# Wider modulation strips and another order for the opening of a two-layer diffusion backbone

## The chip, the cores and the metric

The kernel runs on one core of a Trainium2 chip. A core has a matrix engine (TensorE, with its weight loads), VectorE, ScalarE, GpSimd and SyncE, which mostly issues transfers; the engines run their own instructions in order and wait for each other by semaphores. Transfers from HBM into the on-chip memory (SBUF) run on 16 DMA engines beside them. TensorE writes into PSUM, from where VectorE and ScalarE read. The metric is the device time of one execution in microseconds (us); lower is better.

## The reference

One inference step of two layers over 1024 latent tokens and 128 context tokens of width 1024, all in float32. Every layer starts with the same adaptive modulation:

```python
def ada_modulate(x, cond, norm_g, w_ada, b_ada):
    m = jax.nn.silu(cond) @ w_ada + b_ada
    shift, scale, gate = jnp.split(m, 3, axis=-1)
    h = rms_norm(x, norm_g) * (1.0 + scale[:, None, :]) + shift[:, None, :]
    return h, gate[:, None, :]
```

There are two conditions, one for the latent and one for the context tokens, so `silu(cond) @ w_ada` is a product of 2 rows with a 1024 x 3072 matrix. Layer 0 then projects h by one wide matrix and feeds two head groups: a Conformer convolution (GLU, a depthwise convolution of width 31, LayerNorm, swish) and a neighbourhood attention with the context keys in the same softmax. Their gated outputs go through one output projection. Layer 1 is a pooling mixer with a gate and an output projection. Each layer adds its gated output to its input.

## The kernel before, in words

**Precision.** Large products are made from two parts: a value is rounded to a short form (hi), the rest (lo) is kept, and three matmuls hi·hi, hi·lo and lo·hi stand for one. `split` does this for weights (ScalarE rounds, L186; VectorE subtracts, L187). `h_chunk` (from L442) does it for the modulated input: three transposes on TensorE (L445), scale and shift on ScalarE (L450), the rounding on VectorE (L451), the subtraction on GpSimd for even chunks and on VectorE for odd ones (L452).

**Groups and chunks.** The 9 token tiles of 128 form three groups of 384 tokens: group 0 is tiles 0 to 2, group 1 tiles 3 to 5, group 2 tiles 6, 7 and the context. The width 1024 is 8 chunks of 128 (k). A chain (`chain_ws`, L230) runs over the 8 chunks with three matmuls each into one bank of PSUM. `norm_x` makes the RMS norm of a tile: a Square with a sum on ScalarE (L126), two small steps on GpSimd (L113, L114), a scaling on VectorE (L128).

**Modulation.** The silu of both conditions lies in `sc`, one column for each condition and chunk. Layer 0's shift and scale are made in four steps m = 0 to 3, each for two chunks: `ada0_rows` multiplies four strips of 128 columns of the modulation's weights by the two conditions (L327). The stationary operand is `sc` (2 columns), the moving one the weights, and the four strips run side by side in the array's four groups of 32 columns, so that their results stand in rows 0-1, 32-33, 64-65 and 96-97 of a bank. VectorE copies these rows into `ads` (L333), which was zeroed before; `ada0_cols` transposes it (L338) and makes SH and SC (L273 to L279), which h_chunk needs. The other strips (layer 0's gate and all of layer 1) run later in the background through `ada_strips` (L360) and `ada_cols` (L383, L385, L391).

**The opening.** `first_chains` interleaves the first chains with the loading: the strips m, the chunks T(k, g) of groups 0 and 1, and the chain pieces C(k, ...) for two column blocks of weights x on group 0, written (0, 0) and (1, 0), and for block 0 on group 1, (0, 1). Its order is written out by hand: inside `tc.manual_schedule` TensorE, ScalarE and VectorE run in the program's order. SyncE's and GpSimd's order, and everything outside, is laid out by the planner from its own costs. The first half of the weights' chunks (u = 0, chunks 0 to 3) and the second half (u = 1) are split by `split_w0(c, u)`; the first split stands ahead of this order.

**Buffers that couple steps.** Transposes and strips share two banks of PSUM ("tp"), so a strip or chunk waits until the one before last is read out. The slots of x6 and x7 hold weights of the last modulation step, so these tiles are loaded when the strips of m = 3 have used them.

**Behind the opening** come the remaining projections of layer 0, with the convolution's taps in the background (VectorE L566; ScalarE L553 and GpSimd L555), attention, the output projection, and layer 1.

Of the kernel before, what the change touches and what calls it, by code (L numbers as in the profile page):

```python
# [10 lines left out]
F32 = mybir.dt.float32  # L11
F32R = mybir.dt.float32r
AF = mybir.ActivationFunctionType
ALU = mybir.AluOpType
AX = mybir.AxisListType
P = 128
# [3 lines left out]
G = 384  # L20
# [26 lines left out]
def _body(tc, nc, A, O, const, wp, arena, tmpp, smp, psp):  # L47
# [31 lines left out]

    ident = const.tile([P, P], F32, name="ident")  # L80
    make_identity(nc, ident)
    mhalf = const.tile([P, 16], F32, name="mhalf")
    gp.memset(mhalf, -0.5)
    corr = {}
    for w in (2, 4, 8, 16):
# [19 lines left out]
    xt = {}  # L105
# [35 lines left out]
    se.activation(th0, V[:, :16], AF.Tanh, scale=0.5)  # L141
    cu = small(16, "cu")
    ve.scalar_tensor_tensor(cu, th0, 1.0, V[:, :16], ALU.add, ALU.mult)
    sc = const.tile([P, 8, 2], F32, name="sc")
    ve.tensor_scalar(sc.rearrange("p k c -> p c k"), cu.rearrange("p (c k) -> p c k", c=2), 0.5, None, ALU.mult)

    vq = const.tile([P, 12], F32, name="vq")
    qn8, lgh, lbh = vq[:, 0:1], vq[:, 1:5], vq[:, 5:9]
# [41 lines left out]
    def load_raw0(c, u):  # L190
        wi = A["w_in_0"]
        mem = slot((18, 20)[c], name="raw")[:, :WUNIT] if u else None
        return load_raw([wi[:, c * P : (c + 1) * P], wi[:, 512 + c * P : 512 + (c + 1) * P]], (4 * u,), mem)[0]
# [87 lines left out]

    WAS = (0, 1, 4, 5, 2, 3, 6, 7, 8, 9, 10, 11, 16, 21, 22, 23)
    ads = [const.tile([P, P], F32, name=f"ads{i}") for i in range(2)]
    for t in ads:
        gp.memset(t, 0.0)
    for t in range(3):
        norm_x(t)
    first_w, wt = {}, {}
# [1 line left out]
    def load_wada(m):  # L290
        for kh in range(2):
            for x in range(2):
                t = slot(WAS[4 * m + 2 * kh + x], name="wada")[:, :D].rearrange("p (k c) -> p k c", c=256)
                c0 = x * D + m * 256
                sy.dma_start(t, A["w_ada_0"][kh * 512 : (kh + 1) * 512, c0 : c0 + 256].rearrange("(k p) c -> p k c", p=P))
                wt[m, kh, x] = t
                if m and late:
                    sy.dma_start(*late.pop(0))
# [3 lines left out]
    def split_w0(c, u):  # L302
        first_w[c, u] = split(*raw0[c, u])

    load_wada(0)
    raw0[0, 0] = load_raw0(0, 0)
    raw0[1, 0] = load_raw0(1, 0)
    for t in range(3, 6):
        load_x(t)
    load_wada(1)  # L310
    load_wada(2)
    raw0[0, 1] = load_raw0(0, 1)
    raw0[1, 1] = load_raw0(1, 1)
    load_wada(3)
    for t in (6, 7):
        load_x(t)
    split_w0(0, 0)
    adb = {}

    def ada0_rows(m):  # L320

        b = adb[m] = bank("tp")
        for k in range(8):
            for x in range(2):
                for q in range(2):
                    r = 32 * (2 * x + q)
                    te.matmul(  # L327
                        b[r : r + 2, :P], sc[:, k, :], wt[m, k // 4, x][:, k % 4, q * P : (q + 1) * P],
                        start=(k == 0), stop=(k == 7), tile_position=(0, r),
                    )  # L330
        t = ads[m % 2]
        for r in range(0, P, 32):
            ve.tensor_copy(t[r : r + 2, :], b[r : r + 2, :P])  # L333

    def ada0_cols(m):

# [11 lines left out]
    def ada_strips(l, col, n, fin):  # L348

        st = {}  # L350

        def step(k):
            w = slot(ADS[st_i[0] % len(ADS)], name="wad")[:, : 4 * n]
            st_i[0] += 1
            dma_later(w, A[f"w_ada_{l}"][k * P : (k + 1) * P, col : col + 4 * n])
            if k == 0:
                st["b"] = bank("tp")
            for q in range(4):
                r = 32 * q
                te.matmul(  # L360
                    st["b"][r : r + 2, :n], sc[:, k, :], w[:, q * n : (q + 1) * n],
                    start=(k == 0), stop=(k == 7), tile_position=(0, r),
                )
            if k == 7:
                st["then"] = fin(st["b"])


        then, owed_turn[:] = list(owed_turn), [lambda: st["then"] and st["then"]()]
        adq.append(then + [lambda k=k: step(k) for k in range(4)])
        adq.append([lambda k=k: step(k) for k in range(4, 8)])  # L370
# [8 lines left out]
    def ada_cols(l, b, c0):  # L379

        t = slot(ADS[st_i[0] % len(ADS)], name="adr")[:, :G]
        st_i[0] += 1
        gp.memset(t[:98, :], 0.0)  # L383
        for r in range(0, P, 32):
            ve.tensor_copy(t[r : r + 2, :], b[r : r + 2, :G])  # L385
        return lambda: ada_turn(l, t, c0)

    def ada_turn(l, t, c0):
# [50 lines left out]
        for k in range(8):  # L439
            h_chunk(g, src, l, hs, k, "tp" if k % 2 == 0 else "cv")  # L440

    def h_chunk(g, src, l, hs, k, tag):  # L442
        b = bank(tag)
        for i in range(3):
            te.transpose(out=b[:, i * P : (i + 1) * P], in_=src[i][:, k * P : (k + 1) * P], identity=ident)  # L445
        hi, lo = hsl(hs, 0, k, g), hsl(hs, 1, k, g)
        t = tmp("h")
        for a, e, c in ((0, G, 0),) if g < 2 else ((0, 256, 0), (256, G, 1)):
            s, o = SC[l][:, k, c : c + 1], SH[l][:, k, c : c + 1]
            se.activation(t[:, a:e], b[:, a:e], AF.Identity, bias=o, scale=s)  # L450
        ve.tensor_copy(hi, t[:, :G])  # L451
        (ve if k % 2 else gp).tensor_tensor(lo, t[:, :G], f(hi), ALU.subtract)  # L452

    def hslots(ids):
        return [
            tuple(slot(i, F32R, "h").rearrange("p (k t) -> p k t", t=G) for i in ids[2 * kh : 2 * kh + 2]) for kh in range(2)
        ]

    h0 = {}
# [7 lines left out]
    def first_chains():  # L467


        bs = {(0, 0): (bank("mm"), bank("mm")), (1, 0): (bank("mm"), bank("mm")), (0, 1): (bank("cv"), bank("cv"))}  # L470

        def C(k, which=((0, 0), (1, 0), (0, 1))):
            for x, g in which:
                w = [first_w[x, 0], first_w.get((x, 1))]
                for i in range(2):
                    chain_ws(bs[x, g][i][:, :G], w, i * P, h0, g, ks=(k,))

        def T(k, g):
            h_chunk(g, [xt[t] for t in range(3 * g, 3 * g + 3)], 0, h0, k, "tp")

        h0[0] = hslots(range(4))
        ada0_rows(0)
        ada0_cols(0)
        T(0, 0)
        T(1, 0)
        for k in range(2):
            C(k, ((0, 0),))
        split_w0(1, 0)
        for t in range(3, 6):
            norm_x(t)  # L490
        h0[1] = hslots(range(4, 8))
        for k in range(2):
            C(k, ((1, 0),))
        T(0, 1)
        T(1, 1)
        ada0_rows(1)
        for k in range(2):
            C(k, ((0, 1),))
        ada0_cols(1)
        for k in (2, 3):  # L500
            for g in range(2):
                T(k, g)
        for m in (2, 3):
            ada0_rows(m)
            C(2 * m - 2)
            ada0_cols(m)
            T(2 * m, 0)
            T(2 * m, 1)
            if m == 2:
                split_w0(0, 1)  # L510
            C(2 * m - 1, ((0, 0), (1, 0)))
            T(2 * m + 1, 0)
            T(2 * m + 1, 1)
            if m == 2:
                split_w0(1, 1)
            C(2 * m - 1, ((0, 1),))
        for x in bs:
            for k in (6, 7):
                C(k, (x,))
        return bs  # L520
# [955 lines left out]
```

## Time and profile before

| | us |
|---|---|
| median of 3 runs | 968.03 (967.97 to 968.07) |
| the profiled execution's own time | 967.94 |
| its span in the profile | 966.2 |
| busy in the span: TensorE matmuls | 941.5 |
| VectorE | 603.1 |
| ScalarE | 403.7 |
| GpSimd | 368.9 |

The profile is of one execution. Lines of the profile name an engine (PE is TensorE's matmuls, PEld its weight loads, DVE VectorE, ACT ScalarE, POOL GpSimd, SP SyncE), a line of the kernel, the operation, the tile written and the tiles read, shapes, a count, and in the timeline the start and the duration in us, then in brackets how long the engine had been idle before and what it waited for. A matmul's duration runs to its modelled end and overlaps the next one, so the pace of matmuls is read from their starts. A busy TensorE is therefore also not TensorE at its peak.

### The profile page before, as it was taken

What the parts mean: (1) busy time and instruction counts of PE and PEld (TensorE: products, weight loads), DVE (VectorE), ACT (ScalarE), POOL (GpSimd) and SP (SyncE); (2) the same over time, 40 slices, a digit from 0 to 9 for tenths busy, and PEclk for the clock granted to TensorE, in tenths of its full rate; (3) what the DMA queues carried; (4) which work ended last, traced back from release to release, by engine and by line L of the source; (5) the groups of instructions that cost most, each with busy time, mean ns of one, the idle gap of its engine ahead of it and who ended that gap; (6) DMA issues with size and microseconds to landing.
All of it is one profiled execution on the core that took longest, in us unless ns stands there. A gap on an engine that the chain in (4) does not pass through costs nothing.

```text
span 966.2 us, 16658 instructions
## 1 busy us (share of the span) xinstructions
PE 941.5 (97%) x6388; PEld 864.2 (89%) x6388; DVE 603.1 (62%) x1243; ACT 403.7 (42%) x815; POOL 368.9 (38%) x485
## 2 busy tenths in 40 slices
PE   4999999999999999999999999999999999999998
PEld 2899998899999999987777888889999999998887
DVE  3658999999683444457778447656335455585332
ACT  4365667775611344258876323353222222231010
POOL 2354879999944201125466246530000000004231
PEclk9999999999999999999999999999999999999999
DMA  9956945416111111135344312341111011133211
GB/s 311 308 194 145 363 182 185 160 61 229 47 47 48 47 45 44 45 102 144 111 134 156 131 44 112 103 146 44 55 37 32 32 44 55 66 117 127 106 65 66
DMA packets 87530, 108.53 MB, mean 112 GB/s; under 512 B 10700, under 2 KB 73036, under 8 KB 87339
## 3 DMA queue, kind: packets, MB, share of 16 engines
q1 hardware_dynamic: 82539, 95.93, 31.0%
q0 software_dynamic: 2576, 9.18, 2.4%
q10 hardware_dynamic: 2336, 2.36, 0.7%
q8 instruction: 50, 0.82, 0.4%
q14 instruction: 29, 0.24, 0.1%
HBM read 94.64 MB, written 21.57 MB: 120 GB/s over the span
## 4 chain that ended last, share of the span: by engine, by line
PE 77%; POOL 8%; DVE 5%; ACT 3%; DMA 3%; issue 2%; SPq 1%; ACTq 0%; DVEq 0%; POOLq 0%
PE mm L230 35%; PE mm L1212 10%; PE mm L1205 10%; PE mm L237 8%; POOL zc L555 8%; PE cv L987 3%; PE tp L978 2%; DVE cv L566 2%; PE mm L954 2%; PE mm L1375 2%; PE tp L445 1%; PE cv L230 1%; ACT gr L553 1%; DMA raw<-in_w_out 1%; DVE wlo L187 1%
## 5 line engine op out<-in xcount | busy, mean ns | idle before, releaser
L230 PE MATMUL mm<-h,whi 128*128 128x384 f32 x1504 | 388.5, 338 | 1.0 <-DVE h L451 0.4
L230 PEld LDWEIGHTS mm<-h,whi 128*128 128x128 f32 x1504 | 271.4, 189 | 4.4 <-issue 1.3
L230 PE MATMUL mm<-h,wlo 128*128 128x384 f32 x752 | 252.6, 337 | 0.0
L555 POOL TENSOR_TENSOR zc<-zc,gr 128x384 f32<-128x384 f32 x138 | 148.9, 1080 | 31.8 <-ACT gr L553 23.4
L237 PE MATMUL mm<-whi,h 128*128 128x256 f32 x864 | 156.8, 284 | 1.2 <-DVE qk L731 1.2
L230 PEld LDWEIGHTS mm<-h,wlo 128*128 128x128 f32 x752 | 141.9, 189 | 0.0
L237 PEld LDWEIGHTS mm<-whi,h 128*128 128x128 f32 x864 | 135.1, 192 | 3.3 <-issue 1.4
L237 PE MATMUL mm<-wlo,h 128*128 128x256 f32 x432 | 122.2, 283 | 0.0
L187 DVE TENSOR_TENSOR wlo<-raw,whi 128x1024 fp32r<-128x1024 f32 (+1 forms) x56 | 68.3, 1220 | 47.0 <-ACT whi L186 46.7
L566 DVE SCALAR_TENSOR_TENSOR cv<-u,convw,cv 128x384 f32<-128x384 f32 (+2 forms) x208 | 95.0, 515 | 0.8
L1205 PE MATMUL mm<-whi,zs 128*128 128x512 f32 (+1 forms) x304 | 92.5, 379 | 0.0
L1212 PE MATMUL mm<-wrh,zs 128*128 128x512 f32 x288 | 92.4, 392 | 0.1
L186 ACT CAST whi<-raw 128x1024 fp32r<-128x1024 f32 (+1 forms) x56 | 56.9, 1018 | 64.8 <-PE mm L230 25.4
L237 PEld LDWEIGHTS mm<-wlo,h 128*128 128x128 f32 x432 | 82.9, 192 | 0.0
L1219 POOL TENSOR_TENSOR y<-y,og 128x512 f32<-128x512 f32 x34 | 48.5, 1429 | 84.1 <-DVE og L1217 81.0
L553 ACT ACTIVATE gr<-u,convw 128x384 f32<-128x384 f32 (+2 forms) x128 | 64.5, 532 | 29.5 <-POOL zc L555 29.0
L972 POOL TENSOR_SCALAR p<-p,st 128x512 f32<-128x512 f32 x64 | 48.5, 771 | 47.7 <-DVE st L970 31.2
L1205 PEld LDWEIGHTS mm<-whi,zs 128*128 128x128 f32 x304 | 56.0, 188 | 10.7 <-issue 0.2
L1212 PEld LDWEIGHTS mm<-wrh,zs 128*128 128x128 f32 x288 | 53.9, 188 | 11.7 <-POOL wrh L1181 0.5
L1217 DVE TENSOR_TENSOR og<-mm,gr 128x512 f32<-128x512 f32 x34 | 23.3, 688 | 60.1 <-PE mm L1212 35.6
L535 ACT ACTIVATE th<-mm 128x384 f32<-128x384 f32 x48 | 23.5, 490 | 81.6 <-PE mm L230 81.5
L1205 PE MATMUL mm<-wlo,zs 128*128 128x512 f32 (+1 forms) x152 | 57.2, 378 | 0.0
(215 smaller groups left out, 1393.2 us busy)
## 6 DMA issues: line engine op xcount, KB each, us to landing
raw<-in_w_in SPq DMA_DIRECT2D x28, 512.0 KB
wad<-in_w_ada SPq DMA_DIRECT2D x16, 768.0 KB
wada<-in_w_ada SPq DMA_DIRECT2D x16, 512.0 KB
raw<-in_w_in SPq DMA_DIRECT2D x32, 256.0 KB
raw<-in_w_out SPq DMA_DIRECT2D x16, 512.0 KB
y0scr<-y POOLq DMA_DIRECT2D x9, 512.0 KB, 3.1
y<-y0scr SPq DMA_DIRECT2D x9, 512.0 KB
x<-in_x_sample SPq DMA_DIRECT2D x8, 512.0 KB
```

The lines of the kernel that those rows point to most:

```text
L186: se.copy(hi[:, :n], raw[:, :n])
L187: ve.tensor_tensor(lo[:, :n], raw[:, :n], f(hi[:, :n]), ALU.subtract)
L230: te.matmul(out, wsl(units, a, k, c0, P), hsl(hs, b, k, g), start=(k == 0 and i == 0), stop=(k == nk - 1 and i == 2))
L237: te.matmul(out, hsl(hs, p, k, g, a, P), wsl(units, q, k, 0, 256), start=(k == 0 and i == 0), stop=(k == 7 and i == 2))
L553: se.activation(pr[:, o : o + n], src, AF.Copy, scale=w)
L555: gp.tensor_tensor(z, z, pr, ALU.add)
L566: ve.scalar_tensor_tensor(zp if k == 30 else acc, src, convw[:, c, k : k + 1], zp if k == NPTS[c] else acc, ALU.mult, ALU.add)
L972: gp.tensor_scalar(ps[i][:, e, :], ps[i][:, e, :], st[:, 4 + e : 5 + e], 0.0, ALU.mult, ALU.add)
L987: te.matmul(ob[64 * e : 64 * e + 64, i * P : (i + 1) * P], vw[j0 + i][x][:, 64 * e : 64 * e + 64], pts[i][:, e, n * P : (n + 1) * P], star ...
L1205: te.matmul(b[:, c0 : c0 + n], zs[p][:, k, :], WL[k // 2][q][:, k % 2, c0 : c0 + n], start=(k == 0 and i == 0), stop=(k == 7 and i == 2))
L1212: te.matmul(b, zs[p][:, k, :], WR[q][k // 3][:, k % 3, :], start=(k == 0 and i == 0), stop=(k == 7 and i == 2))
L1219: gp.tensor_tensor(yv, yv, t, ALU.add)
```

## The change

- `sc` is one flat tile of 48 columns, zeroed and then filled, with the two conditions of a chunk side by side. A strip's stationary operand is 32 columns of it from column 2k on, so that a strip writes all 32 rows of its quadrant; rows 0 and 1 are those that are used. One copy of 128 rows takes the place of the four copies of two rows, in the opening and in the later strips, and the memsets of the tiles copied to go away (of `ads`, and one on GpSimd for each `ada_cols`).
- The weights of the second modulation step are loaded ahead of x3 to x5.
- The first split moves into the order written by hand, behind the first step's scales.
- Odd chunks of the opening are rounded on ScalarE and no longer on VectorE.
- In the order of the opening, chunks 0 to 3 of group 0 come first, with the second strips behind chunks 0 and 1; group 1 follows later, and its x tiles are normed behind chunk 3; the second halves of the weights are split sooner with respect to the chains.
- `mhalf` is narrower (8 columns).

```diff
-    sc = const.tile([P, 8, 2], F32, name="sc")
-    ve.tensor_scalar(sc.rearrange("p k c -> p c k"), cu.rearrange("p (c k) -> p c k", c=2), 0.5, None, ALU.mult)
+    sc = const.tile([P, 48], F32, name="sc")
+    gp.memset(sc, 0.0)
+    ve.tensor_scalar(sc[:, :16].rearrange("p (k c) -> p c k", c=2), cu.rearrange("p (c k) -> p c k", c=2), 0.5, None, ALU.mult)
...
-    for t in ads:
-        gp.memset(t, 0.0)
...
+    load_wada(1)
     for t in range(3, 6):
         load_x(t)
-    load_wada(1)
...
-    split_w0(0, 0)
...
-                        b[r : r + 2, :P], sc[:, k, :], wt[m, k // 4, x][:, k % 4, q * P : (q + 1) * P],
+                        b[r : r + 32, :P], sc[:, 2 * k : 2 * k + 32], wt[m, k // 4, x][:, k % 4, q * P : (q + 1) * P],
...
-        t = ads[m % 2]
-        for r in range(0, P, 32):
-            ve.tensor_copy(t[r : r + 2, :], b[r : r + 2, :P])
+        ve.tensor_copy(ads[m % 2], b[:, :P])
...
-                    st["b"][r : r + 2, :n], sc[:, k, :], w[:, q * n : (q + 1) * n],
+                    st["b"][r : r + 32, :n], sc[:, 2 * k : 2 * k + 32], w[:, q * n : (q + 1) * n],
...
-        gp.memset(t[:98, :], 0.0)
-        for r in range(0, P, 32):
-            ve.tensor_copy(t[r : r + 2, :], b[r : r + 2, :G])
+        ve.tensor_copy(t, b[:, :G])
...
-        ve.tensor_copy(hi, t[:, :G])
+        if act:
+            se.copy(hi, t[:, :G])
+        else:
+            ve.tensor_copy(hi, t[:, :G])
```

The new order of the opening, with `one` for both column blocks on group 0 and `two` for block 0 on group 1:

```python
        ada0_rows(0); ada0_cols(0); split_w0(0, 0); T(0, 0); T(1, 0)
        C(0, ((0, 0),)); C(1, ((0, 0),)); split_w0(1, 0); C(0, ((1, 0),)); C(1, ((1, 0),))
        ada0_rows(1); ada0_cols(1); T(2, 0); T(3, 0); norm_x(3), norm_x(4), norm_x(5)
        C(2, one); C(3, one); T(0, 1); T(1, 1)
        ada0_rows(2); C(0, two); ada0_cols(2); split_w0(0, 1); T(2, 1); T(3, 1); C(1, two)
        T(4, 0); T(4, 1); C(2, two); split_w0(1, 1); T(5, 0); T(5, 1); C(3, two); C(4, ((0, 0),))
        ada0_rows(3); C(4, two); ada0_cols(3); C(4, ((1, 0),)); T(6, 0); T(6, 1); C(5, one)
        T(7, 0); T(7, 1); C(5, two)
```

In the old one, the first strips and chunks 0 and 1 of group 0 are followed by the norms of x3 to x5 and chunks 0 and 1 of group 1, then the second strips; from chunk 2 on both groups go side by side.

More of the change, by code (lines that the diff above doesn't have):

```diff
@@ L81, in _body @@
     make_identity(nc, ident)
-    mhalf = const.tile([P, 16], F32, name="mhalf")
+    mhalf = const.tile([P, 8], F32, name="mhalf")
     gp.memset(mhalf, -0.5)
@@ L440, in make_h, with h_chunk @@
             h_chunk(g, src, l, hs, k, "tp" if k % 2 == 0 else "cv")
-    def h_chunk(g, src, l, hs, k, tag):
+    def h_chunk(g, src, l, hs, k, tag, act=False):
         b = bank(tag)
@@ L478, in T @@
         def T(k, g):
-            h_chunk(g, [xt[t] for t in range(3 * g, 3 * g + 3)], 0, h0, k, "tp")
+            h_chunk(g, [xt[t] for t in range(3 * g, 3 * g + 3)], 0, h0, k, "tp", k % 2 == 1)
+        one, two = ((0, 0), (1, 0)), ((0, 1),)
         h0[0] = hslots(range(4))
@@ L483, in first_chains @@
         ada0_cols(0)
+        split_w0(0, 0)
         T(0, 0)
@@ L488, in first_chains @@
         split_w0(1, 0)
+        for k in range(2):
+            C(k, ((1, 0),))
+        ada0_rows(1)
+        ada0_cols(1)
+        T(2, 0)
+        T(3, 0)
         for t in range(3, 6):
@@ L491, in first_chains @@
         h0[1] = hslots(range(4, 8))
-        for k in range(2):
-            C(k, ((1, 0),))
+        C(2, one)
+        C(3, one)
         T(0, 1)
         T(1, 1)
[L496 to L516, printed above, removed]
+        ada0_rows(2)
+        C(0, two)
+        ada0_cols(2)
+        split_w0(0, 1)
+        T(2, 1)
+        T(3, 1)
+        C(1, two)
+        T(4, 0)
+        T(4, 1)
+        C(2, two)
+        split_w0(1, 1)
+        T(5, 0)
+        T(5, 1)
+        C(3, two)
+        C(4, ((0, 0),))
+        ada0_rows(3)
+        C(4, two)
+        ada0_cols(3)
+        C(4, ((1, 0),))
+        T(6, 0)
+        T(6, 1)
+        C(5, one)
+        T(7, 0)
+        T(7, 1)
+        C(5, two)
         for x in bs:
```

## The prediction

> **What bounds the kernel now.** I read the first part of the page, then a table of busy time by stretch, then the waits of TensorE, then the timeline of the first 57 us engine by engine. Start of the page: TensorE is nearly all of the span.
>
> ```profile
> PE 941.5 (97%) x6388; PEld 864.2 (89%) x6388; DVE 603.1 (62%) x1243; ACT 403.7 (42%) x815; POOL 368.9 (38%) x485
> ```
>
> The table by stretch: start and end, length, busy us of TensorE's matmuls, weight loads, VectorE, ScalarE and GpSimd, granted clock, DMA share, GB/s.
>
> ```profile
> 21.00:28.00 7.00, 6.65 (x28) 6.45 (x29) 4.47 (x6) 3.88 (x7) 4.08 (x7) 1.00 1.10 350
> 28.00:46.00 18.00, 16.77 (x218) 14.48 (x220) 12.05 (x27) 7.44 (x12) 5.94 (x5) 1.00 1.07 311
> ...
> 57.00:220.00 163.00, 163.00 (x1216) 150.97 (x1216) 151.59 (x308) 109.66 (x214) 129.19 (x128) 1.00 0.57 189
> 220.00:240.00 20.00, 18.82 (x157) 18.65 (x157) 17.93 (x35) 10.31 (x19) 19.01 (x19) 1.00 0.64 224
> 240.00:420.00 180.00, 180.00 (x1262) 178.96 (x1261) 93.84 (x188) 62.67 (x112) 60.06 (x80) 1.00 0.17 50
> 420.00:540.00 120.00, 116.49 (x1097) 92.78 (x1097) 88.28 (x270) 87.04 (x215) 59.71 (x87) 1.00 0.41 123
> ```
>
> TensorE has no gap from 57 to 220 us and from 240 to 420 us. So what moves the end of the first chains (56 us) moves the end of the kernel by as much, as far as two places allow: the convolution stage up to 236 us, where VectorE (151.59 of 163) and GpSimd (129.19) are nearly full as well, and attention (420 to 540), whose gaps hang on its own steps. In the first place TensorE waited once, behind 57 us:
>
> ```profile
> PE mm L237 <- DVE qk L731: 1.2, 1, 1.2
> ```
>
> That is at 234.6 us. All the rest of the change acts before 57 us, so I follow TensorE through the opening:
>
> ```profile
> 14.24 1.87 PE L327 MATMUL tp<-wada,sc 128*2 128x128 f32 x28 [0.93 <-DMA wada<-in_w_ada]
> 17.49 0.40 PE L338 MATMUL tp<-ident,ads 98*128 98x98 f32 x1 [1.38 <-DVE ads L333]
> ...
> 20.27 0.69 PE L230 MATMUL mm<-h,whi 128*128 128x384 f32 x1 [0.39 <-DVE h L451]
> 21.35 0.69 PE L230 MATMUL mm<-h,whi 128*128 128x384 f32 x1 [0.39 <-POOL h L452]
> ...
> 22.80 0.52 PE L230 MATMUL mm<-h,wlo 128*128 128x384 f32 x1
> ...
> 23.75 0.52 PE L230 MATMUL mm<-h,wlo 128*128 128x384 f32 x1
> ...
> 27.40 0.97 PE L445 MATMUL tp<-ident,x 128*128 128x128 f32 x6
> 28.80 1.93 PE L327 MATMUL tp<-wada,sc 128*2 128x128 f32 x64 [0.43 <-ACT h L450]
> ...
> 32.85 0.25 PE L338 MATMUL tp<-ident,ads 98*128 98x98 f32 x1
> ...
> 35.75 1.93 PE L327 MATMUL tp<-wada,sc 128*2 128x128 f32 x64 [0.26 <-ACT h L450]
> ...
> 38.07 0.33 PE L230 MATMUL mm<-h,wlo 128*128 128x384 f32 x1
> ...
> 38.59 0.33 PE L230 MATMUL mm<-h,wlo 128*128 128x384 f32 x1
> ...
> 45.75 1.93 PE L327 MATMUL tp<-wada,sc 128*2 128x128 f32 x64
> ...
> 55.96 0.51 PE L230 MATMUL mm<-h,whi 128*128 128x384 f32 x2
> ```
>
> From 22.80 to 23.75 lie three chain matmuls, 0.317 us each; from 38.07 to 38.59 again three, 0.173 us each. The granted clock stands at 1.00 in both, so the slow pace of the start is in the records and not in that column. 55.96 is the point I compare by: all chains but chunks 6 and 7 are done there, and what follows is the same in both kernels.
>
> **The change, part by part.** *Start.* These rows of VectorE lie between the first strips (TensorE ends them at 16.11) and the first chunk:
>
> ```profile
> 16.16 1.19 DVE L333 COPY ads<-tp 2x128 f32<-2x128 f32 x4 [4.83 <-PE tp L327]
> 17.38 1.23 DVE L187 TENSOR_TENSOR wlo<-raw,whi 128x1024 fp32r<-128x1024 f32 x1
> 18.63 0.16 DVE L273 TENSOR_TENSOR SH<-tp,V 128x4 f32<-128x4 f32 x1
> ...
> 18.90 0.16 DVE L279 SCALAR_TENSOR_TENSOR SC<-SC,V 128x4 f32<-128x4 f32 x1
> ...
> 28.78 0.36 DVE L451 CAST h<-h 128x384 fp32r<-128x384 f32 x1 [1.13 <-ACT h L450]
> ```
>
> One copy for four leaves 0.30 of the 1.19 us (a copy of 128 rows is bounded by 0.30, the price of one of the four, and 1.19). The split of the first weights (1.23) now comes behind the scales. So: copy done 16.46, transpose 0.14 later and 0.40 long (17.00), scales 0.1 later and 0.43 long (17.55), split to 18.78, rounding 0.36 (19.14), and then GpSimd's low part:
>
> ```profile
> 29.22 1.00 POOL L452 TENSOR_TENSOR h<-h,h 128x384 fp32r<-128x384 f32 x1 [2.36 <-DVE h L451]
> ```
>
> It ends at 20.2; the matmul that waited until 21.35 starts at 20.25, 1.1 us sooner. The 23 matmuls from there took until 27.40, 6.05 us; the same 23 end at 26.3.
>
> *Second strips.* The changed order does them there. Their weights now go ahead of x3 to x5: 2.1 MB at the 350 GB/s of the stretch is 6 us, behind the raw weights that were cast from 20.49 on; they have landed by 26, and I take no wait. At 1.93 us they end at 28.2. Nothing else is ready for TensorE then. Copy (0.05 + 0.30), transpose and its latency (0.4), scales 0.43: 29.4. Then ScalarE and VectorE:
>
> ```profile
> 20.49 1.03 ACT L186 CAST whi<-raw 128x1024 fp32r<-128x1024 f32 x1
> ...
> 22.66 1.06 ACT L126 ACTIVATE gr<-x 128x1024 f32<-128x1024 f32 x1
> ...
> 23.89 1.06 ACT L126 ACTIVATE gr<-x 128x1024 f32<-128x1024 f32 x1
> ...
> 28.08 1.23 ACT L450 ACTIVATE h<-tp,SH,SC 128x384 f32<-128x384 f32 x2 [3.04 <-PE tp L445]
> ...
> 52.20 1.06 ACT L126 ACTIVATE gr<-x 128x1024 f32<-128x1024 f32 x1 [5.49 <-DMA x<-in_x_sample]
> ...
> 53.25 1.22 ACT L450 ACTIVATE h<-tp,SH,SC 128x384 f32<-128x384 f32 x2
> ```
>
> An h is 0.62, the rounding 0.36, the low part 1.00, with 0.3 of latencies: chunk 2 is ready at 31.6. In the old order such a hole is filled by strips or chains of the other group. Here it is 28.2 to 31.6 with six transposes in it.
>
> *The hole and the clock.* The old order has a stretch with transposes alone as well, 32.85 to 35.75, 2.9 us, and the strips behind it kept their fast pace (64 in 1.93 us, where 28 took 1.87 at the start). So I charge no slow matmuls. [...] The price from the rows: 23 matmuls took 6.05 us at the start and would take 4.0 at 0.173; 2 us more, of which the next wait takes back 1.5.
>
> *x3 to x5.* Their Squares now stand on ScalarE behind the two new h and one rounding. That rounding has no row; 384 of the 1024 elements of the cast at 1.03 is 0.4, and I take 0.5 (at most 1.03, at least 0.36, VectorE's price). They start at 31.2. They follow at 1.23 each, and the last one's start lay 3.5 us before the transposes of group 1 (23.89 to 27.40): those come at 31.2 + 2.5 + 3.5 = 37.2. The 24 matmuls of chunks 2 and 3, one of them done, end at 31.6 + 4.0 = 35.6. 1.5 us of TensorE is lost; in the old order the same Squares ran under the 23 matmuls.
>
> *The rest up to the mark,* from 37.1: 60 matmuls at 0.173 (10.4), twelve chunks of transposes at 0.36 (4.4; eight transposes take 0.97 us in the rows below), two strips (3.7), two small transposes (0.2), one wait for a bank as at 27.40 to 28.80 (1.40 less 0.7) and a shorter one (0.5): 19.9, so 57.0. The old mark is 55.96. The opening loses **1.0 us**. The third and fourth strips find their weights: the fourth began at 45.75 in the old order without a wait for them, and starts about 2.5 us later here.
>
> *Roundings on ScalarE.* VectorE gives up eight per group; the chunks that gain by it are odd ones, whose product comes after that of an even one. Nothing on TensorE; if ScalarE were full, 0.5 each.
>
> *Wider strips.* 448 weight loads of 32 columns in place of 2.
>
> ```profile
> 442.20 1.97 PE L987 MATMUL cv<-pt,vw 128*64 128x128 f32 x32
> 444.09 1.09 PE L978 MATMUL tp<-ident,p 128*128 128x128 f32 x8
> 445.06 0.63 PE L978 MATMUL cv<-ident,p 128*128 128x128 f32 x4
> ```
>
> L987 runs pairs of 64 columns with the same 128 moving columns: 32 in 1.89 us, 118 ns for a pair that loads 128 columns. Four strips of 32 load as many; they take 120 ns now (1.93 us for 64). So 0, and at most 1 us in all. The rows behind it give the price of a bare load: eight transposes of 128 columns up to 445.06, 121 ns each, 30 ns for 32 columns.
>
> *Later strips.* They lose two memsets on GpSimd and six of eight copies on VectorE:
>
> ```profile
> L383 POOL MEMSET adr<- x2: 413/414/416, 138.6 to 178.8; 98x384 f32 x2
> L385 DVE COPY adr<-tp x8: 536/552/562, 159.4 to 197.5; 2x384 f32<-2x384 f32 x8
> ```
>
> 0.83 and 3.3 us, ahead of the one wait of 1.2 us at 234.6, which ends with VectorE behind GpSimd. A gain of 0 to 1.2 us; I take 0.5, nearer GpSimd's 0.83 than 3.3, since its queue is the fuller there (19.01 of 20). The new memset of sc lies in GpSimd's idle start and costs nothing.
>
> Sum: +1.0 - 0.5 = +0.5 us. The profiled execution took 967.94 us around its span of 966.2; its median is 968.03, 0.1 above. So 968.5.
>
> **The rivals.** *Faster:* the holes of the new order are no longer than the old ones, because x3 to x5 are normed sooner than I place them. Then the 1.1 us of the start stays, and with the 1.2 us at 234.6 gone the time is 965.7. For it: ScalarE has nothing to do from the second raw cast to 29.4, and x3 to x5 are 1.6 MB, 4.5 us, behind the strips' weights. Against: the order on that engine is written out by hand.
>
> *Slower:* ScalarE is caught by x6. Its Square stood ahead of the h of chunk 6 and waited 5.49 us for the transfer (row 52.20); the h came at 53.25, and transposes of chunk 7 need its bank. That load waits for the fourth strips to free its slot:
>
> ```profile
> 46.83 1.28 SPq L109 DMA_DIRECT2D x<-in_x_sample  x2
> ```
>
> The Square came 6.4 us behind the start of those strips. Here they start at about 48.3, so it would come at 54.7 and h at 55.8, while chunk 7's transposes are due at 55.2 and need until 56.5: 1.3 us, and 0.4 more at chunk 7's first product. With the opening's loss that is +2.7 and no gain later: 970.7. It decides if the Square is again put ahead of chunk 6's h, and x6 lands later than 53.
>
> *The wide loads lie open:* if a load cannot run under a matmul of another strip, 448 x 30 ns are added, 13 us: 981. L987's 118 ns per pair speaks against it. [...]
>
> **How the numbers follow.** Two kernels whose times differ by less than 0.2%, 1.94 us, count as the same here. My forecast, with its unknown terms, 0.57: 967 to 969.9, the same. Faster rival 0.17, of which 0.15 beyond the bound. ScalarE caught by x6, or the clock with it, 0.21; beyond the bound 0.2. Open loads 0.05. What the planner makes of GpSimd's and SyncE's order I can't read; it is in the tails. The range leaves out open loads and the tails of the two others: 965.8 to 971.2.
>
> **What would show it.** In the changed profile: first chain matmul behind the low part near 20.3; second strips at 26 to 28; TensorE idle from there to 31.6 but for transposes; transposes of group 1 near 37; the mark (the first matmul of chunk 6) near 57; the fast pace at 32; 64 strip matmuls still in 1.9 us; the wait at 234 shorter. It is wrong if the mark comes before 55 or after 59, if strips take over 2.5 us, or if the time changes with the mark in place.

## The result, and the profile after

The changed kernel took 973.28 us (median of 4 runs, 972.81 to 974.64), the kernel before 968.05 us beside it (4 runs, 967.97 to 968.68). The ratio is 1.0056, 95% interval 1.0044 to 1.0067: slower by 5.2 us, outside the range. The profiled execution took 974.64 us, the longest of the four, around a span of 972.5.

The rows of TensorE in the opening that answer to those of the prediction (start, us, line, operands, count, idle time before and what ended it):

```profile
20.10 0.69 PE L232 MATMUL mm<-h,whi 128*128 128x384 f32 x1 [0.39 <-POOL h L450]
...
25.71 1.96 PE L326 MATMUL tp<-wada,sc 128*32 128x128 f32 x64
28.08 0.30 PE L335 MATMUL tp<-ident,ads 98*128 98x98 f32 x1 [0.41 <-DVE ads L330]
28.22 1.09 PE L440 MATMUL tp<-ident,x 128*128 128x128 f32 x6
30.05 0.44 PE L232 MATMUL mm<-h,whi 128*128 128x384 f32 x1 [0.73 <-DVE h L449]
31.13 0.44 PE L232 MATMUL mm<-h,whi 128*128 128x384 f32 x1 [0.64 <-POOL h L450]
31.41 0.34 PE L232 MATMUL mm<-h,wlo 128*128 128x384 f32 x1
...
36.45 0.66 PE L440 MATMUL tp<-ident,x 128*128 128x128 f32 x4 [0.84 <-DVE x L128]
37.54 1.96 PE L326 MATMUL tp<-wada,sc 128*32 128x128 f32 x64 [0.43 <-ACT h L445]
...
54.73 0.49 PE L440 MATMUL tp<-ident,x 128*128 128x128 f32 x3
56.61 0.55 PE L440 MATMUL tp<-ident,x 128*128 128x128 f32 x3 [1.39 <-ACT h L445]
...
58.05 0.51 PE L232 MATMUL mm<-h,whi 128*128 128x384 f32 x2
```

The start came as forecast (20.10 for 20.25), so did the hole (chunk 2's first matmul runs at 30.05, the second waits for GpSimd's low part until 31.13, and the rest follow from 31.41; forecast 31.6) and the transposes of group 1 (the last four at 36.45; forecast 37.2). The strips with 32 columns took 1.96 us, against 1.93 with two. The mark stands at 58.05, 2.09 behind the old one; 1.39 of that is the wait at 56.61. ScalarE shows what it waited for:

```profile
54.85 1.06 ACT L126 ACTIVATE gr<-x 128x1024 f32<-128x1024 f32 x1 [1.65 <-DMA x<-in_x_sample]
55.81 0.19 ACT L126 ACTIVATION_READ_ACCUMULATOR gr<-x 128x1 f32 x1
55.90 0.65 ACT L445 ACTIVATE h<-tp,SH,SC 128x384 f32<-128x384 f32 x1
```

The Square of x6 stands ahead of the second h of chunk 6 and waits for its transfer. This is the slower rival, at its place (forecast: Square 54.7, h 55.8).

The other 3 us come later. Both kernels issue 6388 matmuls, so they can be numbered and the starts of equal numbers subtracted. The difference is 2.1 us at the mark, between 1.8 and 2.6 up to 75 us and 2.2 to 2.3 from there to 236 us; it grows by 1.47 there, by 0.54 at 266.3, by about 0.3 in attention and by 1.6 at 872. The waits of TensorE from 57 us on, and the busy time of TensorE, its loads, VectorE, ScalarE and GpSimd from 220 to 240 us:

```profile
PE mm L239 <- DVE qk L741: 3.0, 2, 2.6
```

```profile
220.00:240.00 20.00, 17.36 (x145) 17.18 (x145) 19.11 (x35) 9.68 (x17) 17.86 (x17) 1.00 0.83 277
```

So the wait that I expected to shrink from 1.2 us grew to 2.6, with 0.4 more at 266.3. TensorE waits there for VectorE to read out a bank (L731, now L741), and VectorE for a small step on GpSimd, which stands in GpSimd's queue among the additions of the convolution. VectorE's rows, before and after:

```profile
234.61 0.42 DVE L731 TENSOR_TENSOR qk<-mm,rstd 128x256 f32<-128x256 f32 x1 [0.19 <-POOL rstd L114]
```

```profile
238.88 0.75 DVE L741 TENSOR_TENSOR qk<-mm,rstd 128x256 f32<-128x256 f32 x2 [0.46 <-POOL rstd L114]
```

The wait at 872 is for the last output weights, which the same order of issues brought 1.6 us later in this execution. That is about how far this execution lies above its median (1.4), and other profiles here show that wait between none and 1.2 us; I count it as scatter.

### The profile page after: what moved, and what is told of

Its sections match the earlier page's. It is cut to its first block, busy times and chain, and to the rows that moved or that the text cites. A ratio compares the mean times of both kernels' runs of the same rounds, so it can differ in the third digit from the quotient of the medians.

```text
span 972.5 us, 16624 instructions
## 1 busy us (share of the span) xinstructions
PE 942.0 (97%) x6388; PEld 866.4 (89%) x6388; DVE 592.7 (61%) x1217; ACT 407.3 (42%) x823; POOL 367.8 (38%) x482
## 4 chain that ended last, share of the span: by engine, by line
PE 74%; POOL 11%; DVE 5%; ACT 4%; issue 3%; DMA 3%; SPq 0%; POOLq 0%; DVEq 0%; ACTq 0%
PE mm L232 35%; PE mm L1222 10%; PE mm L1215 10%; POOL zc L565 9%; PE mm L239 5%; PE cv L997 3%; DVE cv L576 2%; PE tp L988 2%; PE mm L964 2%; PE mm L1385 2%; ACT gr L563 1%; DMA wada<-in_w_ada 1%; DMA raw<-in_w_out 1%; POOL rstd L114 1%; PE tp L440 1%
## 5 line engine op out<-in xcount | busy, mean ns | idle before, releaser
L576 DVE SCALAR_TENSOR_TENSOR cv<-u,convw,cv 128x384 f32<-128x384 f32 (+1 forms) x208 | 95.7, 513 | 1.2
L1215 PEld LDWEIGHTS mm<-whi,zs 128*128 128x128 f32 x304 | 56.0, 188 | 11.2 <-ACT whi L188 0.6
```

Source lines behind the costliest of these rows:

```text
L576: ve.scalar_tensor_tensor(zp if k == 30 else acc, src, convw[:, c, k : k + 1], zp if k == NPTS[c] else acc, ALU.mult, ALU.add)
L1215: te.matmul(b[:, c0 : c0 + n], zs[p][:, k, :], WL[k // 2][q][:, k % 2, c0 : c0 + n], start=(k == 0 and i == 0), stop=(k == 7 and i == 2))
```

## The experiments

Eleven kernels ran, each timed beside the kernel before on the same chip. For each profile I took three differences from the profile before, in us: how much later the 451st matmul starts (61.77 us in the kernel before), how much later GpSimd's additions of the convolution ("taps"; ScalarE scales what they add) run near 200 us, and how much later the 1851st matmul starts (246.89 us), behind the convolution stage.

| kernel | ratio, 95% interval | 451st matmul | taps near 200 us | 1851st matmul |
|---|---|---|---|---|
| changed kernel | 1.0056, 1.0044 to 1.0067 | +2.1 | +4.6 | +3.7 |
| strips_only | 1.0011, 1.0002 to 1.0020 | +1.6 | +1.2 | +0.6 |
| order_only | 1.0049, 1.0036 to 1.0062 | +3.0 | +6.8 | +3.7 |
| after_x67_last | 1.0051, 1.0038 to 1.0064 | +0.6 | +5.2 | +4.4 |
| after_x345_early | 1.0109, 1.0096 to 1.0122 | +7.5 | +10.5 | +11.2 |
| after_bias3 | 1.0018, 1.0009 to 1.0027 | +1.5 | +1.3 | +0.6 |
| after_x67_bias3 | 0.9991, 0.9982 to 1.0000 | +1.1 | +0.2 | -0.2 |
| before_bias3 | 0.9985, 0.9976 to 0.9994 | +1.0 | -1.5 | -0.5 |
| strips_x67_bias3 | 0.9996, 0.9987 to 1.0005 | -0.3 | -3.7 | -0.9 |
| before_raw_late2 | 1.0076, 1.0063 to 1.0089 | +0.2 | +3.1 | +5.9 |
| before_raw_late3 | 1.0064, 1.0052 to 1.0077 | +0.7 | +4.4 | +6.7 |
| after_filled_x67_bias3 | 1.0007, 0.9998 to 1.0016 | +1.3 | +0.9 | +0.1 |

The differences are of one execution each. Three of these kernels (before_bias3 and the two late loads) have the opening of the kernel before, and their 451st matmul starts 0.2 to 1.0 us later all the same, so that less than 1 us in one of these columns says little.

Runs also differ in the mean granted clock of TensorE. It is 0.999 or 1.000 in all four runs of the changed kernel and in 64 of the 65 that the experiments have of the kernel before. As an estimate, 0.001 of a span of 970 us is 1 us, so a run at 0.996 has lost up to 4 us to a slow clock; where a kernel's runs had less than 0.999, the text says so if it matters.

**The parts of the change, and its opening.** The first theory was that the opening loses the time: the holes of the new order and x6's Square. The first four kernels take the change apart.

*strips_only*: the kernel before with the wide strips alone (sc of 48 columns, one copy, no memsets).

```diff
-                        b[r : r + 2, :P], sc[:, k, :], ...
+                        b[r : r + 32, :P], sc[:, 2 * k : 2 * k + 32], ...
...
-        for r in range(0, P, 32):
-            ve.tensor_copy(t[r : r + 2, :], b[r : r + 2, :P])
+        ve.tensor_copy(ads[m % 2], b[:, :P])
```

> The kernel before, in its old order, with only the wide strips: 32 columns of sc, one copy for four, no memsets. Theory: the order of the opening costs all of the 5.2 us and the strips cost nothing; the first scales come 0.9 us sooner, and GpSimd and VectorE are relieved by 0.8 and 3.3 us before 236 us, so 966.5 to 968.1 us, with the 64 strip matmuls in 1.9 to 2.0 us. Rival A, open weight loads: slower than before by 1 us or more, 969 to 973. Rival B, the planner lays everything behind the edit out anew and the loss is its chance: anything between 966 and 971, with the mark (first matmul of chunk 6) where it was at 56.0 and the difference behind 57 us.

Measured 969.73 us beside 969.10 for the kernel before on that chip, ratio 1.0011: not the gain of the theory, and by the interval at most 2 us of the loss, so neither the wide loads nor the copies are its main cause. Its transposes of chunk 7 wait 1.05 us behind x6's Square as well, and of the wait near 236 us 0.2 is left.

*order_only*: the changed kernel with strips of two columns, four copies and the memsets again.

```diff
-                        b[r : r + 32, :P], sc[:, 2 * k : 2 * k + 32], ...
+                        b[r : r + 2, :P], sc[:, k, :], ...
...
-        ve.tensor_copy(ads[m % 2], b[:, :P])
+        t = ads[m % 2]
+        for r in range(0, P, 32):
+            ve.tensor_copy(t[r : r + 2, :], b[r : r + 2, :P])
```

> The changed kernel with the old strips (2 columns, four copies, memsets). Theory: the order alone loses; 973 to 975 us, with the mark at 58 to 59 us and the wait at 235 us at 2.5 us or more. Rival A, the wide strips cost the loss: 968 to 970 us. Rival B, chance of the planner's layout: mark near 58, the wait at 235 us may be anything from 0 to 4 us.

Measured 973.9 us, ratio 1.0049: the order of the opening carries most of the loss. How much is less sure than the ratio looks. Four of the six runs had a granted clock of 0.996 and took 973.5 to 975.7 us; the two at 1.000 took 971.5 and 972.6, which is 2.4 and 3.5 us above the kernel before on that chip. The wait near 235 us was 1.5 us in the profile (one of the two), not 2.5 or more.

*after_x67_last*: the changed kernel, x6 and x7 normed at the end of the first chains.

```diff
                 C(k, (x,))
+        for t in (6, 7):
+            norm_x(t)
         return bs
```

> The changed kernel with the norms of x6 and x7 written at the end of the opening's order, so that their Squares can't stand ahead of the h of chunks 6 and 7 on ScalarE. Theory: the wait of 1.4 us in the transposes of chunk 7 goes, the mark comes at 56.6 us in place of 58.05, and the taps of the convolution start sooner by as much or more, so 970.5 to 972 us. Rival, the Square is hidden and the hole behind the second strips is the whole cause: the mark stays within 0.3 us of 58.05 and the time at 972.8 to 973.8.

Measured 974.32 us, ratio 1.0051. The mark and the waits of TensorE between 225 and 270 us:

```profile
56.57 0.51 PE L232 MATMUL mm<-h,whi 128*128 128x384 f32 x2
```

```profile
PE mm L239 <- DVE qk L743: 3.9, 3, 3.0
```

The mark came back by 1.48 us, as expected, and the time did not: TensorE arrived sooner and waited 3.9 us in place of 3.0. The median has slow matmuls in it (three of its five runs at 0.996 to 0.998 of the clock), but the profiled execution stood at 1.000 and took 974.54 us. The theory of the opening falls with this. Up to 236 us something else sets the time.

*after_x345_early*: the changed kernel, x3 to x5 normed ahead of the second strips.

```diff
         split_w0(1, 0)
+        for t in range(3, 6):
+            norm_x(t)
...
         T(3, 0)
-        for t in range(3, 6):
-            norm_x(t)
```

> The changed kernel with the norms of x3 to x5 moved on all engines' order to where the old kernel had them, behind the second raw split and ahead of the second strips' scales. Theory: the transposes of group 1 no longer wait for the Squares (1.0 us idle ahead of them goes), but x3 to x5 land behind the second strips' weights, so h of chunk 2 may come up to 1 us later: the mark at 57 to 58, 971.8 to 973.3 us. Rival, the norms' place is the whole loss of the opening: mark at 56, 970.5 us or less. Rival, ScalarE is caught by x5's landing: mark later than 58.5, 974 us or more.

Measured 979.4 us, ratio 1.0109, which is where the last rival put it, though the wait came by VectorE. The Squares of x3 to x5 started between 25.29 and 28.93 us in place of 30.61 to 32.97 in the changed kernel, and the first two waited 4.69 and 1.20 us for their transfers. The strips had ended at 27.96 us, but on VectorE the scaling of x5 ran ahead of their copy:

```profile
31.20 0.75 DVE L128 TENSOR_SCALAR x<-x,rstd 128x1024 f32<-128x1024 f32 x1 [0.71 <-POOL rstd L114]
31.87 0.28 DVE L330 COPY ads<-tp 128x128 f32<-128x128 f32 x1
```

```profile
32.21 0.42 PE L335 MATMUL tp<-ident,ads 98*128 98x98 f32 x1 [4.25 <-DVE ads L330]
```

So TensorE stood still for 4.25 us, and behind that its matmuls ran at about half pace for 8.8 us, until 41.0. A part of the slow stretch, in the columns that the prediction's table has (the seventh is the granted clock):

```profile
34.00:40.80 6.80, 5.98 (x18) 5.58 (x19) 0.96 (x2) 1.18 (x2) 1.00 (x1) 0.50 1.08 302
```

At half pace, 8.8 us are a loss of up to 4.4 of the 10.3 by which this kernel is slower. Written sooner, the norms were held by their transfers, and held up the strips.

**The convolution stage.** What holds it up shows in three queues of the changed kernel. First SyncE's DMA issues, then ScalarE, then GpSimd:

```profile
85.46 1.33 SPq L214 DMA_DIRECT2D raw<-in_w_in  x2
86.83 4.44 SPq L802 DMA_DIRECT2D tbias<-in_rpb  x3
91.31 2.30 SPq L266 DMA_DIRECT2D wad<-in_w_ada  x1
95.56 0.88 SPq L802 DMA_DIRECT2D tbias<-in_rpb  x1
96.49 1.18 SPq L214 DMA_DIRECT2D raw<-in_w_in  x2
```

```profile
94.01 0.68 ACT L563 ACTIVATE gr<-u,convw 128x128 f32<-128x128 f32 x2
100.76 1.05 ACT L188 CAST whi<-raw 128x1024 fp32r<-128x1024 f32 x1 [6.07 <-DMA raw<-in_w_in]
```

```profile
94.47 2.69 POOL L565 TENSOR_TENSOR zc<-zc,gr 128x384 f32<-128x384 f32 x2 [10.13 <-ACT gr L563]
103.02 3.21 POOL L565 TENSOR_TENSOR zc<-zc,gr 128x384 f32<-128x384 f32 x3 [5.87 <-ACT gr L563]
```

```profile
90.21 1.22 DVE L189 TENSOR_TENSOR wlo<-raw,whi 128x1024 fp32r<-128x1024 f32 x1
```

```profile
SPq L802 <- DMA tbias<-in_rpb: 1.9, 1, 1.9
```

The last two are VectorE's row that frees the second pair's buffer, and a wait of SyncE. The raw weights of the last channel block come in two pairs of transfers. VectorE lets go of the second pair's buffer at 91.4, but the pair is issued at 96.49, behind four fills of the bias table, which serves attention, and one load of modulation weights; the last fill waited 1.9 us for an earlier one. Its cast waits 6.07 us. Behind it in ScalarE's queue stand the scalings that GpSimd's taps need, and GpSimd stands still for 5.87. In the kernel before, the pair is issued at 91.30, and the two casts that wait are these (before the change):

```profile
93.31 1.05 ACT L186 CAST whi<-raw 128x1024 fp32r<-128x1024 f32 x1 [2.86 <-DMA raw<-in_w_in]
95.51 1.05 ACT L186 CAST whi<-raw 128x1024 fp32r<-128x1024 f32 x1 [0.45 <-DMA raw<-in_w_in]
```

In the kernel before the pair stands behind fills as well: its buffer is free at 87.2, 4.1 us ahead of the issue. So of the 5.2 us by which the pair is issued later, only 1.0 comes from SyncE's queue; 4.2 come from the buffer, whose split on VectorE ends at 91.4 in place of 87.2, behind a cast that waits 4.00 us for TensorE in place of 2.06.

The second theory looked at that queue: the new order of the opening moves the planner's order on SyncE's queue, raw weights come late, and the convolution stage is held up until TensorE waits for it near 236 us. By the figures above the queue holds the pair back in both kernels, by 4.1 and 5.1 us, and most of the difference between them is the buffer. To test it, the bias table is built two items later in the program's main loop, out of the way of the raw weights:

```diff
-        if i == 1:
+        if i == 3:
             bias_table()
```

*after_bias3*: this in the changed kernel.

> The changed kernel, but the bias table, whose fills SyncE issues at 95.56 us ahead of the second pair of raw weights at 96.49, is built two taps of the loop later. Theory (the convolution stage sets the time up to 236 us, and it is held up there because ScalarE's cast of the raw weights waits 6.07 us for its transfer at 100.76): the pair is issued before 94 us, the cast waits at most 3 us, GpSimd's taps stand at most 3.5 us behind the kernel before from 105 us on (4.7 in the changed kernel), TensorE's wait near 236 falls from 2.8 us to 1.5 or less, and the time is 970.5 to 971.5. Rival (the cast's wait only takes up time in which GpSimd would have waited for TensorE's products anyway): the cast waits less, the taps stay 4.5 us or more behind, the time stays 973 to 974.

Measured 970.36 us, ratio 1.0018. Both pairs are issued in one go, the casts do not wait, and TensorE's wait near 236 is nearly gone:

```profile
85.08 5.73 SPq L214 DMA_DIRECT2D raw<-in_w_in  x4
```

```profile
93.04 1.98 ACT L188 CAST whi<-raw 128x1024 fp32r<-128x1024 f32 x2
```

```profile
PE mm L239 <- DVE qk L741: 0.4, 1, 0.4
```

The buffer of the second pair is free at 89.9, still 2.7 us later than in the kernel before, and the pair is issued at once. Every number of the theory came but the time, which is a little below its 970.5 to 971.5. The opening is 0.6 us less late.

*after_x67_bias3*: with the norms of x6 and x7 last as well.

> The changed kernel with the norms of x6 and x7 at the end of the first chains, which took the first matmul of chunk 6 back to 0.6 us behind the kernel before without changing the time, and with the later bias table. Theory (two causes in a row: the opening's 2.1 us are felt only if the convolution stage doesn't hide them, and that stage is held up by the raw weights): now both are gone, TensorE is 0.7 us behind at 220 us, waits at most 1.5 us near 236, and the time is 969 to 970.5. Rival (the raw weights are not what holds the convolution stage up): 973 to 974.5 as with the norms moved alone.

Measured 967.57 us, ratio 0.9991, somewhat below the expected 969 to 970.5. The four ratios of the two edits say how the two causes stand to each other: 1.0056 with neither, 1.0051 with the norms moved alone, 1.0018 with the table moved alone, 0.9991 with both. The norms are worth 0.05% while the raw weights are late and 0.27% once they are not. In this version's profile GpSimd has 1% of the chain that ended last, against 8% before the change and 11% in the changed kernel:

```profile
PE 93%; DMA 2%; DVE 2%; issue 1%; ACT 1%; POOL 1%; SPq 0%; DVEq 0%; ACTq 0%; POOLq 0%
```

*before_bias3*: the table moved in the kernel before.

> The kernel before with the later bias table alone. In it both pairs of raw weights are issued ahead of the table's fills already (87.23 and 91.30 us), and the cast waits 2.86 and 0.45 us. Theory: nothing to gain there, 967.5 to 968.5. Rival (the later table is good or bad by itself, since its DMAs and its operations on VectorE fall elsewhere): a change of over 1 us, by which the two runs above would have to be corrected.

Measured 967.57 us beside 968.79 for the kernel before on that chip, ratio 0.9985: "nothing to gain" was wrong, and so was the reason, since the fills do stand ahead of both pairs in the kernel before. The move by itself is worth 0.15%, against 0.38% in the changed kernel, so 0.23% (2.2 us) of that belong to the changed kernel's own lateness. The taps run 1.5 us sooner, since ScalarE's waits of 2.86 and 0.45 us go as well. This version is faster than both kernels, by a little: 0.06 to 0.24% below the kernel before.

*strips_x67_bias3*: the old order with the wide strips and both moves.

> The kernel before with the wide strips (old order), the norms of x6 and x7 at the end of the first chains, and the later bias table. The strips alone lost 1.55 us at the transposes of chunk 7, which waited for the h behind x6's Square, and took away the wait at 234 us (1.34 us before). Theory: the loss at chunk 7 goes, the wait at 234 stays away, 966.5 to 968. Rival (the norms of x6 and x7 now stand behind the first chains and hold up what follows them on ScalarE and VectorE): 969 to 971, with the taps of GpSimd over 1 us behind from 70 us on.

Measured 968.3 us, ratio 0.9996, just above the theory's range. The loss at chunk 7 and the wait near 236 are gone and TensorE is 0.9 us ahead at 246.89, but 1.2 us go to the wait for the last output weights. No gain that can be measured.

**The reverse: late raw weights in the kernel before.** If the theory holds, the kernel before must lose as much when nothing is changed but the landing of that second pair. It is loaded twice or three times, each load over the last:

```diff
-                sy.dma_start(raw..., s...)
+                for _ in range(again if k0 else 1):
+                    sy.dma_start(raw..., s...)
...
-                raws[j] = load_raw(items[j][0])
+                raws[j] = load_raw(items[j][0], again=3 if j == 3 else 1)
```

> The kernel before with nothing changed but one thing: the second pair of raw weights that it loads at 91.30 us is loaded twice, the second time over the first. The opening and the orders of the engines stay. Theory (a late pair of raw weights holds up ScalarE, its tap scalings, GpSimd and so TensorE near 236 us): the second cast, which waited 0.45 us at 95.51, waits 3 to 4 us; GpSimd's taps are 2 to 3.5 us behind from 103 us on; TensorE's wait near 236 grows from 1.2 to 3.5 to 4.5 us; time 2 to 3.5 us above the kernel before on the same chip. Rival (the convolution stage takes the delay up, and the changed kernel loses its time otherwise): the cast waits, the time is within 1 us of the kernel before.

> As the run above, with the pair loaded three times. Theory: the cast waits 6 to 8 us, as in the changed kernel (6.07); GpSimd's taps are 5 to 6.5 us behind from 103 us on, TensorE's wait near 236 is 6 to 7.5 us, and the time is 4.5 to 6.5 us above the kernel before: the whole loss of the changed kernel, with its opening untouched. Rival: within 1 us of the kernel before.

Measured 975.37 and 974.01 us, ratios 1.0076 and 1.0064: the loss of the changed kernel and more, with an opening that is 0.2 and 0.7 us late. So a late pair alone is enough for the loss, and the rival is out. The repeat itself holds up little else in SyncE's queue: with two loads the next raw weights are issued at 99.60 us, not later than in the kernel before (100.35). With the pair loaded twice, the cast and TensorE's waits were these:

```profile
100.98 1.05 ACT L186 CAST whi<-raw 128x1024 fp32r<-128x1024 f32 x1 [5.40 <-DMA raw<-in_w_in]
```

```profile
PE mm L238 <- ACT gr L554: 3.8, 1, 3.8
...
PE mm L238 <- DVE qk L732: 1.0, 1, 1.0
```

The sizes were missed. The cast waited 5.40 us, not 3 to 4, and TensorE lost more than GpSimd was late by (5.9 against 3.1 us). One part of that shows: behind the single wait of 3.8 us the clock dropped. TensorE's row behind it, and the stretches by time (busy us, then granted clock, DMA share, GB/s):

```profile
236.36 0.56 PE L238 MATMUL mm<-whi,h 128*128 128x256 f32 x1 [3.77 <-ACT gr L554]
```

```profile
236.00:239.50 3.50, 3.14 (x15) 3.17 (x16) 3.39 (x7) 1.81 (x4) 3.26 (x5) 0.53 0.14 39
239.50:243.00 3.50, 2.49 (x20) 2.31 (x20) 2.23 (x5) 1.69 (x4) 3.34 (x4) 0.98 0.00 0
```

Fifteen matmuls took 0.21 us each, against 0.12 ahead of the wait (from 227.75 us), 1.4 us in all. With three loads ScalarE did other work first (its cast waited 6.08 us, at 108.24) and TensorE was 2.6 us behind at 146 us already; near 236 it waited 1.5 and 1.9 us, not 6 to 7.5, and the mean granted clock of its profiled execution was 0.998. Why two loads cost no less than three is settled in part: the mean granted clock was 0.996 to 0.998 in the five runs with two loads and 0.997 to 1.000 in those with three, a difference of the means worth up to 1.7 us by the estimate above, and the two medians lie 1.4 us apart.

**The hole.** *after_filled_x67_bias3*: as after_x67_bias3, with the second strips ahead of two products of the second column block.

```diff
         split_w0(1, 0)
-        for k in range(2):
-            C(k, ((1, 0),))
         ada0_rows(1)
+        C(0, ((1, 0),))
         ada0_cols(1)
         T(2, 0)
+        C(1, ((1, 0),))
         T(3, 0)
```

> The version with the moved norms of x6 and x7 and the later bias table, in which TensorE no longer waits near 236 us, with the hole behind the second strips filled: those strips and their columns go ahead of the products of chunks 0 and 1 for the second column block. Theory (where GpSimd is not behind, what moves the opening moves the end by as much): the hole of 2 us shrinks to under 0.6, the first matmul of chunk 6 comes 1 to 2 us sooner than in that version, and so does the end: 965.5 to 967, 1 to 2 us below the version without it. Rival (the strips' weights have not landed so early, or the convolution stage becomes the bound): TensorE waits for the weights near 23 us or near 236 us for what it gained, and the time stays 967 to 968.

Measured 968.53 us, ratio 1.0007: not faster. The strips ran at 23.56 without a wait, and of the hole a wait of 0.6 us was left; the 201st matmul stood 1.4 us ahead of the version without the edit. Then the third strips went at half pace:

```profile
36.70 3.62 PE L326 MATMUL tp<-wada,sc 128*32 128x128 f32 x64 [0.43 <-ACT h L445]
```

```profile
36.70:40.30 3.60, 3.60 (x65) 3.22 (x65) 1.09 (x2) 1.97 (x3) 1.00 (x1) 0.53 0.91 277
```

So the gain of 1.4 us was given back by a loss of 1.7: filling one hole opened the next (33.5 to 36.7, transposes of group 1 that wait for x3 to x5), and the clock dropped there. That was not this execution alone: 7 of the 11 runs had a mean granted clock of 0.998 or less, none of the kernel before beside them. Neither the theory's 1 to 2 us nor the rival's waits came.

## Why the prediction was wrong

**Right:** the start, the second strips, the hole, the transposes of group 1, the price of the wide strips, all within 1 us of the forecast. The roundings were not tried alone. The opening without x6 loses 0.6 us (after_x67_last), where +1.0 was forecast.

**The term that was mis-sized: the mark.** It came at 58.05, not 57.0. The 1.39 us behind x6's Square more than make the difference, which the prediction had as the slower rival, with the right times and with 0.21 for its chance (shared with the clock). Its price at the end was read wrongly, though: taking it away moved the mark and not the time, as long as the raw weights were late.

**The step that failed: "So what moves the end of the first chains (56 us) moves the end of the kernel by as much", and with it "A gain of 0 to 1.2 us; I take 0.5" for the wait at 234.6 us.** The prediction did name the convolution stage as a place that could limit the step, but it priced it as a gain alone. The table shows both ends of the failure. Where the taps are late by 1.3 us or less, the wait of the kernel before takes the first 1.0 to 1.3 us of a late opening (strips_only: +1.6 becomes +0.6). Where they are late, the opening doesn't matter (after_x67_last: +0.6 becomes +4.4; the two late loads: +0.2 and +0.7 become +5.9 and +6.7). I priced the convolution stage by the work it loses, 0.83 and 3.3 us of memsets and copies, and took its timing as moving along with the mark. Its work did go down; its order and its transfers came later, and that cost more: +3.7 us at 246.89 in the changed kernel and +0.6 once the bias table is out of the way (after_bias3). The prediction said that the planner's order of GpSimd and SyncE "is in the tails": it was the largest term.

The profile had a line that spoke against the step, and I did not read it, the chain that ended last. Before, and after the change:

```profile
PE 77%; POOL 8%; DVE 5%; ACT 3%; DMA 3%; issue 2%; SPq 1%; ACTq 0%; DVEq 0%; POOLq 0%
```

```profile
PE 74%; POOL 11%; DVE 5%; ACT 4%; issue 3%; DMA 3%; SPq 0%; POOLq 0%; DVEq 0%; ACTq 0%
```

GpSimd carried 8% of it, some 77 us. TensorE was busy beside it, so no gap of TensorE showed them; only the wait at 234.6 did, which I took for slack to be gained. It was the sign that another chain had arrived last. Followed in time, that chain passes through the second pair of raw weights in the kernel before already (start, us, what):

```profile
91.97 3.47 DMA raw<-in_w_in
95.51 1.05 ACT whi L186
...
234.61 0.42 DVE qk L731
```

In the changed kernel it passes through the same pair, at 97.17 us; in before_bias3 it is TensorE alone from 84 to 245 us.

**The clock.** The prediction charged no slow matmuls for the hole, and in the profiled execution there were none. In those of after_bias3 and after_x67_bias3, with the same hole, there were; 3 and 5 of their 11 runs had a mean granted clock of 0.998 or less. So the 2 us that the prediction priced and did not charge are lost in some executions. This row is of after_bias3:

```profile
31.00:34.50 3.50, 3.35 (x11) 3.35 (x12) 1.57 (x3) 3.08 (x6) 2.12 (x6) 0.53 1.14 327
```

Eleven matmuls, which at 0.173 us take 1.9 of these 3.5 us: a loss of 1.6 us that comes or not from execution to execution.

**Open** is why the second pair's buffer came free 4.2 us later in the changed kernel, when TensorE was only 2.2 us behind, and why the planner put the table's fills ahead of the raw weights, in both kernels; that they stood there, and what a late pair costs, is shown. The parts of the change don't add up to its loss either: strips_only and the two runs of order_only at full clock lose 0.6 and 2.4 to 3.5 of the 5.2 us. Nor is it shown how much of the first 2.86 us wait in the kernel before could still be had.

## What to carry to other kernels

An engine with no gap is not yet the bound: ask the chain that ended last, and where an engine at 97% waits even once, ask which chain arrived there and what that one hangs on, before you count the wait as slack. When an order is changed by hand and the rest is planned by a program, list the orders of the other engines and of the DMA queues far behind the edit too; here a table that was not needed for a long time went ahead of weights that a casting engine was about to wait for, in the kernel before too, where it cost only 0.15%. Two causes that meet in one wait hide each other: removing the one that comes first shows nothing (0.05% here) until the other is gone (0.27%), so try the pair, and put the suspected delay into the good kernel as well.

## What the runs showed of the hardware

- A transfer's lateness reached work that doesn't use it: in the changed kernel ScalarE's cast waited 6.07 us for the raw weights, and GpSimd's taps 5.87 us for the scalings behind that cast.
- The pace of TensorE fell to half behind some waits, and the column of the granted clock shows it: 0.53 for 3.5 us behind a wait of 3.77 us (before_raw_late2) and 0.50 from 34.0 to 40.8 us behind one of 4.25 (after_x345_early). The profiled execution of after_x67_last, with a wait of 3.0, has a mean of 1.000. Behind the new order's hole, which has transposes in it, it fell in some executions (from 31.0 to 34.5 us 0.53 in after_bias3 and 0.56 in after_x67_bias3) and not in others (1.00 in the changed kernel from 31 to 35 us). The slow stretch at the start (until 25.4 us in the profile before, with 0.317 us for a chain matmul against 0.173 later) stands at 1.00 in that column, so a 1.00 there doesn't rule it out. Its end was not the same in all profiles: it lay between 23 and 25.4 us in six (before, the changed kernel, order_only, after_x67_last, after_x345_early, after_filled_x67_bias3), and in two others (after_bias3, after_x67_bias3) the matmuls were fast at 20.3 us, slow from about 21 to 24.4 (granted clock 0.52 from 21.0 to 24.5 us in after_x67_bias3) and fast again.
- 64 strip matmuls with 32 columns of weights took 1.96 us at full pace in the changed kernel and 1.95 in after_x345_early, against 1.93 with two columns (the kernel before, order_only).
